# RWKV's sums over head channels on four groups of TensorE columns, and spreads through DRAM in place of matmuls

## The chip, the cores and the metric

The kernel runs on one core of a Trainium2 chip. The metric is the device time of one execution in microseconds (us). Below, PE is TensorE, DVE is VectorE, ACT is ScalarE, POOL is GpSimd and SP is SyncE, which here only issues DMAs. PEld is TensorE's loading of weights, which runs beside its matmuls.

## The reference

One decoder layer on x of 1024 tokens by 1024 channels, float32. After an RMS norm, one projection feeds two branches: an RWKV-7 time mixing (8 heads of 64 channels) and a sparse attention (8 heads of 64 channels, 256 keys for each query, chosen by an indexer). Their outputs are merged through sigmoid gates and followed by a SwiGLU FFN and a last norm. What the change touches:

```python
kk = (k * k_k).reshape(B, S, H, N)
kk = kk / jnp.maximum(jnp.linalg.norm(kk, axis=-1, keepdims=True), 1e-12)
...
bonus = jnp.sum(r_h * k_h * r_k, axis=-1, keepdims=True) * v_h
...
prob = jax.nn.softmax(logits, axis=-1)
return jnp.einsum('bqhk,bqkhd->bqhd', prob, vg)
```

The first is a sum of squares over the 64 channels of a head, for each token, whose inverse root multiplies all 64 channels again. The second is a sum over the same 64 channels that multiplies v's channels. The third divides the attention's output of a head by its softmax sum. All three are sums per head and token that have to be spread back over 64 channels. Channels lie on partitions here, two heads in each of four tiles of 128 channels, and tokens lie along the free dimension.

## The kernel before

Tokens are worked in two halves of 512; the RWKV branch works in four quarters of 256 tokens (q = 0 to 3, two in each half). Projections and FFN matmuls are float32 products made of three passes (mm3, L138, L139, L143): weights and activations are split into a high and a low part (split, L112 on ACT and L113 on DVE), and 24 matmuls of 512 columns make one output tile.

TensorE's order is written out by hand; the order on the other engines comes from the scheduler of the tile framework. A queue of generators, fill, holds the projection, gate, attention, merge and FFN work as small pieces; pump(n) takes n matmuls' worth of it and puts it into TensorE's queue at that place, so that it covers the latency of what stands around it. ticks(n, m) does the same in m parts. rwkv(half, ...) calls pump between its own steps with numbers for each quarter. In a quarter, in this order:

- L525 multiplies the decay and the in-context rate up, L529 takes their tanh on ACT, L536 scans the log decays on DVE, L540 and L542 exponentiate them on ACT (P and Pi).
- kk is scaled k, sq its square (L556). L561 sums sq over a head's channels: eight matmuls with sq as the stationary operand and the two-column indicator ind2 as the moving one, so that sums come with tokens on partitions. L564 bounds them from below, L566 raises them to the power -1/2 on POOL, L570 transposes them back (two transposes), L572 splits them into a high and a low part (nrT), and L579 spreads them over the channels with eight matmuls by the indicator ind8. L581 multiplies kk by the result in PSUM.
- L589 transposes v. AR (L597, L598) holds kk and r times decays, BK (L604, L607) the in-context rate times kk, and k, times inverse decays. rk (L612) is the product for the bonus.
- L622 sums and spreads rk at once, with the block matrix blk (128 by 128, ones where two channels are of one head); L623 multiplies v by the result in PSUM (bon).
- In q = 2, ready() then runs what is left of fill (the end of the attention of half 0), frees its buffers and puts the merge of half 0 into fill; the merge reads d_ya and d_yb back and splits them (L1095, L1096).
- L639 multiplies BK and AR into MT, L643 masks it on DVE, L658 transposes BK. Then follow a triangular solve on DVE, beside which ticks pumps fill, and the chunk recurrence; its end (finish) adds bon.

The attention (attend) works on units of a pair of heads and 128 queries. When a pair's four units are done, close1 takes the reciprocal of the softmax sums (ri), close2 spreads them over channels with eight matmuls against the identity (L1030) and copies the result to SBUF (L1033), and close3 multiplies the attention's output, still in PSUM, by it (L1037) and writes it to d_yb. close2 and close3 come one unit apart.

DMAs: SP carries RWKV's loads and stores and, outside RWKV, the weights; during RWKV the weights go through ACT's queue (wq). Each queue issues in order, and an issue that waits holds up those behind it.

Of the kernel before, what the change touches and what calls it, by code (L numbers as in the profile page):

```python
# [24 lines left out]
HT = 512  # L25
# [20 lines left out]
K_ID, K_ONE, K_CAUS, K_BO = range(4)  # L46
# [3 lines left out]
def block_kernel(ctx: ExitStack, tc: tile.TileContext, ins: dict, outT: bass.AP, stop=None, dbg=None):  # L50
# [30 lines left out]
    smp.tile([128, 40], F32, name="edge")  # L81
# [15 lines left out]
    d_yb = scratch("d_yb", [4, 128, HT])  # L97
    d_n = [dp.tile([64, 32, 32], F32, name=f"d_n{q}") for q in range(4)]
# [371 lines left out]
    def rwkv_consts(p):  # L470
        blk = p.tile([128, 128], F32, name="blk")
        SY.dma_start(blk, ins["consts"][:, K_BO, :])
# [6 lines left out]
        ind8 = p.tile([8, 512], F32R, name="ind8")  # L479
        t = tmp()  # L480
        SY.dma_start(t[0:8, :], ins["ind8"])
        A.activation(ind8, t[0:8, :], AF.Copy)
# [7 lines left out]
        ind2 = smp.tile([128, 2], F32, name="ind2")  # L490
        SY.dma_start(ind2, ins["ind2"])

        return blk, cmask, wup, gup, rmask, ind2, ind8

    def rwkv(half, p, consts, ready=None):
        blk, cmask, wup, gup, rmask, ind2, ind8 = consts
# [4 lines left out]
        for q in range(2 * half, 2 * half + 2):  # L501
# [43 lines left out]


# [10 lines left out]
            pump((30, 16, 16, 20)[q])  # L557
            ps = mix()
            for t in range(2):
                for ct in range(4):  # L560
                    T.matmul(ps[:, t * 8 + ct * 2:t * 8 + ct * 2 + 2], sq[:, ct, t * 128:(t + 1) * 128], ind2,  # L561
                             start=True, stop=True)
            nr = p.tile([128, 16], F32, tag="nr", name="nr")
            V.tensor_scalar(nr, ps[:, 0:16], 1e-24, None, op0=ALU.max)  # L564
# [4 lines left out]
            for t in range(2):  # L569
                T.transpose(ps[0:8, t * 128:(t + 1) * 128], nr2[:, t * 8:(t + 1) * 8], ident)  # L570
            nrT = p.tile([8, 2, 256], F32R, tag="rhs", name="nrT")
            split(nrT[:, 0, :], nrT[:, 1, :], ps[0:8, 0:256])  # L572
            pump(10)
            for c in range(2):
                ps = mix()
                for e in range(2):
                    ct = 2 * c + e
                    for i in range(2):
                        T.matmul(ps[:, e * 256:(e + 1) * 256], ind8[:, ct * 128:(ct + 1) * 128], nrT[:, i, :],  # L579
                                 start=i == 0, stop=i == 1)  # L580
                V.tensor_tensor(kk[:, 2 * c:2 * c + 2, :], kk[:, 2 * c:2 * c + 2, :],  # L581
                                ps.rearrange("p (c t) -> p c t", c=2), op=ALU.mult)
# [10 lines left out]

            kk4 = kk.rearrange("p c (n t) -> p c n t", n=4)
# [4 lines left out]
            V.tensor_scalar(ta, ta, 0.5, 0.5, op0=ALU.mult, op1=ALU.add)  # L599
            V.tensor_tensor(ta, ta, kk, op=ALU.mult)  # L600
            BK = [p.tile([128, 2, 2, 4, 64], F32, tag=f"BK{c}", name="BK") for c in range(2)]
            for c in range(2):
                s2 = slice(2 * c, 2 * c + 2)
                V.tensor_tensor(BK[c][:, :, :, 1:3, :].rearrange("p c r s t -> p (c r) (s t)"),  # L604
                                ta[:, s2, :].rearrange("p c (r t) -> p (c r) t", r=2),
                                Pi[:, s2, :].rearrange("p c (r t) -> p (c r) t", r=2), op=ALU.mult)
                V.tensor_tensor(BK[c][:, :, :, 0:4:3, :].rearrange("p c r s t -> p (c r) s t"),  # L607
                                km[:, s2, :].rearrange("p c (r s t) -> p (c r) s t", r=2, s=2),
                                Pi[:, s2, :].rearrange("p c (r s t) -> p (c r) s t", r=2, s=2), op=ALU.mult)
            rk = t4("x6")  # L610
            for ct in range(4):
                V.scalar_tensor_tensor(rk[:, ct, :], r[:, ct, :], par[:, P_RK + ct:P_RK + ct + 1], km[:, ct, :],  # L612
                                       op0=ALU.mult, op1=ALU.mult)


            bon = v
            pump((28, 38, 32, 32)[q])
            for c in range(2):
                ps = mix()
                for e in range(2):  # L620
                    ct = 2 * c + e
                    T.matmul(ps[:, e * 256:(e + 1) * 256], blk, rk[:, ct, :], start=True, stop=True)  # L622
# [333 lines left out]
    def attend(half, p, bias):  # L956
# [64 lines left out]
        def close1(sm):  # L1021
            ri = smp.tile([128, 4, 2], F32, tag="ri", name="ri", bufs=2)
            V.reciprocal(ri, sm)
            return ri

        def close2(ri):
            pb = mix()
            for bi in range(4):
                for e in range(2):
                    T.matmul(pb[64 * e:64 * e + 64, bi * 128:(bi + 1) * 128], ri[:, bi, e:e + 1].to_broadcast([128, 64]),  # L1030
                             ident, start=True, stop=True)
            rb = tmp()
# [383 lines left out]
```

## Time and profile before

| | |
|---|---|
| median of 3 runs | 1779.17 us (1772.55 to 1781.16) |
| the profiled execution | 1776.56 us, span 1774.8 us |
| mean granted clock of TensorE | 0.993 |
| instructions | 26838 |
| DMA | 244.00 MB, mean 137 GB/s |

The span runs from the first to the last instruction of the profiled execution; the execution's own time is a little longer. Busy time is the time in which an engine has at least one instruction under way. In the profile, a group or timeline row names the line of the kernel, the engine, the operation, what it writes and reads, the shape and the count; a bracket at the end of a timeline row tells how long the engine had been idle and which instruction released it. A float32 matmul stands in the profile as two records. Rows by window give, for each engine, its busy time and count, then TensorE's granted clock, the DMA engines' share and GB/s. In the rows of DMA issues the last number is the median time from issue to landing. In groups, the last column is the engine's idle time just before, and who ended it.

### The profile page before, as it was taken

The numbers are of one execution on the slowest core, as the hardware profiler recorded it, in microseconds if no ns is written. First come the engines' busy times: TensorE is split into PE (matmuls) and PEld (weight loads), VectorE is DVE, ScalarE is ACT, GpSimd is POOL, SyncE is SP. The second block draws the span as 40 slices with busy tenths as digits, with TensorE's granted clock in tenths as the row PEclk, the third lists the DMA queues.
The fourth block names the chain that finished last, engine by engine and source line by source line (L and its number), as shares of the span: only waits on it lengthen the run. The fifth ranks groups of instructions, "written<-read, shape, count | busy, mean of one in ns | idle before, by whom it ended". The sixth has DMA issues, their size and how long they took to land. (4 is left out here: it accounts for less than half of the span.)

```text
span 1774.8 us, 26838 instructions
## 1 busy us (share of the span) xinstructions
PE 1731.5 (98%) x10256; PEld 1432.1 (81%) x10256; DVE 1117.6 (63%) x2137; ACT 832.2 (47%) x1535; POOL 93.5 (5%) x120
## 2 busy tenths in 40 slices
PE   7999999999999999999999999999999999999997
PEld 6888888788888777777888888888788888888877
DVE  5779989866468568847865655524565564454464
ACT  6355998453444788654233455523334322232231
POOL 0000000010021110001000311000000000000000
PEclk9999999999999999999999999999999999999999
DMA  5542224536375535723244854243565344434441
GB/s 207 165 138 90 101 95 143 164 86 176 92 203 171 148 108 173 227 88 110 78 119 113 240 154 119 76 139 112 185 206 154 108 135 148 143 97 156 129 139 64
DMA packets 130992, 244.00 MB, mean 137 GB/s; under 512 B 36536, under 2 KB 59704, under 8 KB 130736
## 3 DMA queue, kind: packets, MB, share of 16 engines
q1 hardware_dynamic: 107472, 168.38, 30.7%
q10 hardware_dynamic: 15552, 47.75, 8.8%
q0 software_dynamic: 7840, 26.15, 5.6%
q8 instruction: 81, 1.33, 0.3%
q14 instruction: 47, 0.39, 0.1%
HBM read 189.29 MB, written 52.95 MB: 136 GB/s over the span
## 5 line engine op out<-in xcount | busy, mean ns | idle before, releaser
L113 DVE TENSOR_TENSOR wlo<-wst,whi 128x1024 fp32r<-128x1024 f32 (+1 forms) x231 | 277.8, 1204 | 306.1 <-PE acc L143 139.7
L112 ACT ACTIVATE whi<-wst 128x1024 fp32r<-128x1024 f32 (+1 forms) x231 | 240.6, 1043 | 282.3 <-PE acc L139 224.0
L138 PE MATMUL acc<-zhi,whi 128*128 128x512 f32 x672 | 265.8, 396 | 1.3 <-DVE tmp L1189 1.3
L139 PE MATMUL acc<-zlo,whi 128*128 128x512 f32 x672 | 262.8, 391 | 0.0
L143 PE MATMUL acc<-zhi,wlo 128*128 128x512 f32 x672 | 170.1, 392 | 0.0
L138 PEld LDWEIGHTS acc<-zhi,whi 128*128 128x128 f32 x672 | 126.8, 189 | 28.5 <-issue 3.4
L138 PE MATMUL acc<-fhi,whi 128*128 128x512 f32 (+1 forms) x400 | 145.0, 371 | 3.9 <-ACT fhi L112 3.9
L139 PEld LDWEIGHTS acc<-zlo,whi 128*128 128x128 f32 x672 | 126.8, 189 | 25.0
L143 PEld LDWEIGHTS acc<-zhi,wlo 128*128 128x128 f32 x672 | 124.8, 188 | 25.5 <-issue 0.7
L139 PE MATMUL acc<-flo,whi 128*128 128x512 f32 (+1 forms) x400 | 143.7, 367 | 1.4 <-DVE flo L113 1.2
L138 PE MATMUL acc<-u1hi,whi 128*128 128x512 f32 x352 | 140.5, 399 | 0.1
L138 PE MATMUL acc<-u0hi,whi 128*128 128x512 f32 (+1 forms) x352 | 135.3, 387 | 4.2 <-DVE tmp L281 2.4
L139 PE MATMUL acc<-u1lo,whi 128*128 128x512 f32 x352 | 137.6, 391 | 0.0
L139 PE MATMUL acc<-u0lo,whi 128*128 128x512 f32 (+1 forms) x352 | 133.7, 382 | 0.0
L143 PE MATMUL acc<-fhi,wlo 128*128 128x512 f32 (+1 forms) x400 | 92.6, 369 | 0.0
L138 PEld LDWEIGHTS acc<-fhi,whi 128*128 128x128 f32 x400 | 76.1, 190 | 17.9 <-ACT fhi L112 5.8
L143 PE MATMUL acc<-u1hi,wlo 128*128 128x512 f32 x352 | 89.7, 394 | 0.0
L139 PEld LDWEIGHTS acc<-flo,whi 128*128 128x128 f32 x400 | 76.2, 190 | 14.6 <-DVE flo L113 3.3
L143 PE MATMUL acc<-u0hi,wlo 128*128 128x512 f32 (+1 forms) x352 | 86.0, 384 | 0.0
L112 ACT ACTIVATE fhi<-tmp 128x512 fp32r<-128x512 f32 x44 | 27.8, 631 | 113.7 <-DVE tmp L1169 113.7
L138 PEld LDWEIGHTS acc<-u0hi,whi 128*128 128x128 f32 x352 | 66.1, 188 | 17.5 <-issue 2.6
L143 PEld LDWEIGHTS acc<-fhi,wlo 128*128 128x128 f32 x400 | 69.6, 191 | 12.1 <-issue 0.5
(304 smaller groups left out, 3146.0 us busy)
## 6 DMA issues: line engine op xcount, KB each, us to landing
wst<-in_w_ffn_in SPq DMA_DIRECT2D x72, 512.0 KB, 3.7
wst<-in_w_in ACTq DMA_DIRECT2D x36, 512.0 KB, 3.7
wst<-in_w_in SPq DMA_DIRECT2D x27, 512.0 KB, 3.7
wst<-in_w_fo SPq DMA_DIRECT2D x25, 512.0 KB, 3.7
k<-d_k POOLq DMA_DIRECT2D x24, 512.0 KB, 8.3
h<-in_xT SPq DMA_DIRECT2D x32, 256.0 KB, 5.2
d_g<-tmp ACTq DMA_DIRECT2D x32, 256.0 KB, 3.0
tmp<-d_g SPq DMA_DIRECT2D x32, 256.0 KB, 3.1
```

Of the source, the lines that this page charges most:

```text
L112: A.activation(hi, x, AF.Copy)
L113: V.tensor_tensor(lo, x, hi.bitcast(F32), op=ALU.subtract)
L138: T.matmul(ps, whi[:, wk + k, :], ahi[:, ak + k, tok], start=k == 0, stop=False)
L139: T.matmul(ps, whi[:, wk + k, :], alo[:, ak + k, tok], start=False, stop=False)
L143: T.matmul(ps, wlo[:, wk + k, :], ahi[:, ak + k, tok], start=False, stop=k == nk - 1)
```

## The change

Five things are done.

1. The sums over a head's channels, of sq and of rk, are made by one helper, sums(x): four matmuls with the indicator ind (128 by 32, two columns of which count) as the stationary operand, one for each tile of channels, into the rows 32 ct to 32 ct + 31 of one PSUM tile. So each uses its own 32 of TensorE's 128 columns.
2. The sums of sq are copied to SBUF (nq, on ACT), transposed by two matmuls, bounded and raised to the power on POOL as before, transposed again (16 rows), copied (nt), written to DRAM (d_kn) and read back with a broadcast over 64 partitions, once for each head parity, into the half of AR that isn't in use yet (nrs). One DVE instruction multiplies kk by nrs. AR's kk and r products come after it.
3. The sums of rk are copied to SBUF (bs), written to DRAM (d_bs), and read back with a broadcast into P's buffer once AR is made. One DVE instruction makes bon from v and it, and stands after the loads of the triangular solve.
4. In the softmax closing, close2 transposes ri (one matmul), copies it and the attention's output to SBUF and writes the sums to DRAM (d_s); a new close3 reads them back with a broadcast; close4 multiplies. So a closing takes three steps instead of two. The last pair of heads of half 0 keeps the matmuls.
5. The matmuls by ind2, ind8 and blk and the split of nrT are gone, ready() stands behind the sums of rk and ahead of AR, and the numbers of the pumps are others: a quarter pumps 16 more in all ahead of L639.

```diff
+            def sums(x):
+                ps = mix()
+                for ct in range(4):
+                    T.matmul(ps[32 * ct:32 * ct + 32, 0:256], ind, x[:, ct, :], start=True, stop=True)
+                return ps[:, 0:256]
...
             pump((30, 16, 16, 20)[q])
+            ps = sums(sq)
+            nq = p.tile([128, 2, 128], F32, tag="rhs", name="nq")
+            A.activation(nq.rearrange("p a b -> p (a b)"), ps, AF.Copy)
+            pump(4)
             ps = mix()
             for t in range(2):
-                for ct in range(4):
-                    T.matmul(ps[:, t * 8 + ct * 2:t * 8 + ct * 2 + 2], sq[:, ct, t * 128:(t + 1) * 128], ind2,
-                             start=True, stop=True)
+                T.transpose(ps[:, t * 128:(t + 1) * 128], nq[:, t, :], ident)
...
             G.tensor_tensor(nr2, nr, mhalf, op=ALU.pow)
             pump((34, 36, 30, 30)[q])
             ps = mix()
-            for t in range(2):
-                T.transpose(ps[0:8, t * 128:(t + 1) * 128], nr2[:, t * 8:(t + 1) * 8], ident)
-            nrT = p.tile([8, 2, 256], F32R, tag="rhs", name="nrT")
-            split(nrT[:, 0, :], nrT[:, 1, :], ps[0:8, 0:256])
-            pump(10)
-            for c in range(2):
-                ps = mix()
-                for e in range(2):
-                    ct = 2 * c + e
-                    for i in range(2):
-                        T.matmul(ps[:, e * 256:(e + 1) * 256], ind8[:, ct * 128:(ct + 1) * 128], nrT[:, i, :],
-                                 start=i == 0, stop=i == 1)
-                V.tensor_tensor(kk[:, 2 * c:2 * c + 2, :], kk[:, 2 * c:2 * c + 2, :],
-                                ps.rearrange("p (c t) -> p c t", c=2), op=ALU.mult)
+            T.transpose(ps[0:16, 0:128], nr2, ident)
+            nt = p.tile([16, 128], F32, tag="rhs", name="nt")
+            A.activation(nt, ps[0:16, 0:128], AF.Copy)
+            SY.dma_start(d_kn[q].rearrange("e c (t s) -> (e c t) s", t=2), nt)
+            nrs = AR.rearrange("p c n s t -> p (c n s t)")[:, 1024:2048]
+            for e in range(2):
+                SY.dma_start(nrs[64 * e:64 * e + 64, :],
+                             d_kn[q][e].rearrange("c s -> (c s)").partition_broadcast(64))
...
+            rk = t4("x6")
...
+            pump((10, 12, 10, 10)[q])
+            bs = tmp()
+            A.activation(bs[:, 0:256], sums(rk), AF.Copy)
+            for e in range(2):
+                SY.dma_start(d_bs[q][e], bs[e::32, 0:256])
+            if q == 2:
+                ready()
...
+            V.tensor_tensor(kk.rearrange("p c t -> p (c t)"), kk.rearrange("p c t -> p (c t)"), nrs, op=ALU.mult)
             kk4 = kk.rearrange("p c (n t) -> p c n t", n=4)
...
-            pump((28, 38, 32, 32)[q])
-            for c in range(2):
-                ps = mix()
-                for e in range(2):
-                    ct = 2 * c + e
-                    T.matmul(ps[:, e * 256:(e + 1) * 256], blk, rk[:, ct, :], start=True, stop=True)
-                V.tensor_tensor(bon[:, 2 * c:2 * c + 2, :], v[:, 2 * c:2 * c + 2, :],
-                                ps.rearrange("p (c t) -> p c t", c=2), op=ALU.mult)
-
-            if q == 2:
-                ready()
+            pump((40, 48, 44, 44)[q])
...
+            bsp = t4("P")
+            for e in range(2):
+                SY.dma_start(bsp[64 * e:64 * e + 64].rearrange("p c t -> p (c t)"),
+                             d_bs[q][e].rearrange("c s -> (c s)").partition_broadcast(64))
+            bon = v
+            V.tensor_tensor(bon, v, bsp, op=ALU.mult)
             ticks((255, 240, 285, 245)[q], (13, 4, 10, 6)[q])
...
+            T.transpose(pb[0:8, 0:128], ri.rearrange("p e b -> p (e b)"), ident)
+            y = p.tile([128, HT], F32, tag="y", name="y")
+            rt = tmp()
+            A.activation(rt[0:8, 0:128], pb[0:8, 0:128], AF.Copy)
+            A.activation(y, py, AF.Copy)
+            SY.dma_start(d_s[half][hp].rearrange("e (b t) -> (e b) t", b=4), rt[0:8, 0:128])
+            return None, y
+
+        def close3(x, hp):
+            rb, y = x
+            if rb is None:
+                rb = tmp()
+                for e in range(2):
+                    SY.dma_start(rb[64 * e:64 * e + 64, :], d_s[half][hp][e].partition_broadcast(64))
+            return rb, y
```

More of the change, by code (lines that the diff above doesn't have):

```diff
@@ L43 @@
 NPAR = 66
-K_ID, K_ONE, K_CAUS, K_BO = range(4)
+K_ID, K_ONE, K_CAUS = range(3)
 @with_exitstack
@@ L1021, in close1 @@
         def close1(sm):
-            ri = smp.tile([128, 4, 2], F32, tag="ri", name="ri", bufs=2)
-            V.reciprocal(ri, sm)
-            return ri
-        def close2(ri):
-            pb = mix()
-            for bi in range(4):
-                for e in range(2):
-                    T.matmul(pb[64 * e:64 * e + 64, bi * 128:(bi + 1) * 128], ri[:, bi, e:e + 1].to_broadcast([128, 64]),
-                             ident, start=True, stop=True)
-            rb = tmp()
-            A.activation(rb, pb, AF.Copy)
-            return rb
@@ L1036, in close3, with close2 @@
-        def close3(rb, py, hp):
-            V.tensor_tensor(rb, py, rb, op=ALU.mult)
-            SY.dma_start(d_yb[half][hp], rb)
+            ri = smp.tile([128, 2, 4], F32, tag="ri", name="ri", bufs=2)
+            V.reciprocal(ri.rearrange("p e b -> p b e"), sm)
+            return ri
+        def close2(ri, py, hp):
+            pb, rb = mix(), None
+            if half == 0 and hp == 3:
+                for bi in range(4):
+                    for e in range(2):
+                        T.matmul(pb[64 * e:64 * e + 64, bi * 128:(bi + 1) * 128],
+                                 ri[:, e, bi:bi + 1].to_broadcast([128, 64]), ident, start=True, stop=True)
+                rb = tmp()
+                A.activation(rb, pb, AF.Copy)
+                return rb, py
+            T.transpose(pb[0:8, 0:128], ri.rearrange("p e b -> p (e b)"), ident)
[5 more added lines that the diff above has]
+            return None, y
```

73 lines of the change are left out of this document (37 added, 36 removed).

## Prediction

> **What bounds the kernel now.** I read the page first, for its busy shares and its chain.
>
> ```profile
> span 1774.8 us, 26838 instructions
> PE 1731.5 (98%) x10256; PEld 1432.1 (81%) x10256; DVE 1117.6 (63%) x2137; ACT 832.2 (47%) x1535; POOL 93.5 (5%) x120
> PE 25%; issue 1%; DVE 1%; DMA 1%; ACT 0%; POOLq 0%; POOL 0%; DVEq 0%; ACTq 0%
> ```
>
> TensorE is busy for 98% of the span, and the part of the chain that could be followed back is TensorE too. Its order is written out by hand, and the projection matmuls (the fill) keep it busy between other steps. So the whole time is TensorE's work plus the time in which it waits. A matmul taken out of its queue is a gain of its own length, and each microsecond in which the head of its queue waits is lost. The other engines count only where TensorE waits for them.
>
> **What TensorE no longer does.** Next I read TensorE's timeline around the touched steps of the second quarter (q = 1); the columns are start, length, engine, line.
>
> ```profile
> 510.70 0.39 PE L139 MATMUL acc<-u1lo,whi 128*128 128x512 f32 x1
> ...
> 511.61 0.39 PE L139 MATMUL acc<-u1lo,whi 128*128 128x512 f32 x1
> 511.83 1.84 PE L561 MATMUL mix<-ind,AR 128*128 128x2 f32 x16
> 513.53 0.49 PE L138 MATMUL acc<-u1hi,whi 128*128 128x512 f32 x1
> ```
>
> ```profile
> 521.84 0.38 PE L570 MATMUL mix<-kc,nr 128*8 128x128 f32 x2
> 521.98 1.17 PE L143 MATMUL acc<-u1hi,wlo 128*128 128x512 f32 x4
> ...
> 524.88 1.09 PE L579 MATMUL mix<-nrT,ind 8*128 8x256 f32 x7 [0.53 <-DVE nrT L113]
> 525.90 1.09 PE L589 MATMUL mix<-kc,v 128*128 128x128 f32 x8
> 526.75 0.47 PE L138 MATMUL acc<-u1hi,whi 128*128 128x512 f32 x1
> ```
>
> ```profile
> 535.33 1.89 PE L622 MATMUL mix<-x,blk 128*128 128x256 f32 x8
> 537.15 4.29 PE L639 MATMUL mix<-AR,BK 64*128 64x128 f32 x64
> 541.37 1.97 PE L658 MATMUL mix<-kc,BK 128*128 128x128 f32 x16
> 543.09 0.48 PE L138 MATMUL acc<-u1hi,whi 128*128 128x512 f32 x1
> ```
>
> Lengths overlap in the pipeline, so I count from start to start. A fill matmul takes 0.91/4 = 0.228. L561 takes 1.70, L570 0.14, L579 1.02 for 7 and so 1.17 for 8, L622 1.82: 4.83 us in a quarter go. What comes is three transposes (two like L589's, 0.85/8 = 0.106 each, one like L570's, 0.07; 0.28 together) and two sums, of k squared and of rk, on four column groups. One sum has the records of L622: 8 of 256 columns. No row shows four groups; the softmax spread shows two.
>
> ```profile
> 575.95 1.04 PE L1030 MATMUL mix<-kc,ri 128*64 128x128 f32 x16
> 576.92 0.74 PE L993 MATMUL mix<-k,q 128*128 128x512 f32 x2
> ```
>
> 16 records of 128 columns take 0.97, 0.061 each, against half of L622's 0.228, 0.114, with no groups: two groups work almost twice as fast. A sum then costs between 1.82/4 = 0.46 and 1.82 (no overlap at all). I take 0.96, the speed of the nearest row. A quarter saves 4.83 - 1.92 - 0.28 = 2.63, four save 10.5 (3.6 to 14.5). Seven of eight softmax closings replace L1030 by one transpose: 7 x (0.97 - 0.07) = 6.3. **Term a: -16.8** (-20.8 to -9.9).
>
> [...] Ahead of and behind L1030's two-group run the starts above hide at most about 0.1 us each; 16 such borders would be 1.6 us, inside the bounds of term a.
>
> **Waits that go.** TensorE's groups by line, then three stretches of 3.4 us in the last quarter:
>
> ```profile
> L579 PE MATMUL mix<-nrT,ind 8*128 8x256 f32 x32 | 6.4, 331 | 3.0 <-DVE nrT L113 2.9 <-ACT nrT L112 0.2
> L138 PE MATMUL acc<-yhi,whi 128*128 128x512 f32 x128 | 50.7, 396 | 3.3 <-ACT yhi L112 2.0 <-DVE h L1189 1.3
> L658 PE MATMUL mix<-kc,BK 128*128 128x128 f32 x64 | 8.4, 279 | 0.7 <-DVE MT L643 0.7
> ```
>
> ```profile
> 840.50:843.90 3.40, 1.50 (x6) 0.76 (x5) 3.40 (x6) 1.07 (x3) 0.00 (x0) 1.00 0.07 27
> 843.90:847.30 3.40, 3.18 (x14) 2.96 (x15) 2.92 (x7) 0.24 (x1) 0.00 (x0) 0.50 0.54 157
> 847.30:850.70 3.40, 3.40 (x11) 2.72 (x10) 3.40 (x6) 2.13 (x4) 0.00 (x0) 0.50 0.02 5
> ```
>
> The split of nrT goes, and its 3.0 us of waiting. In the stretches TensorE is busy for 1.50 of 3.40 us (the long wait for nrT), and the clock granted after it is 0.50 for two stretches: about 3.2 us more. **Term b: -6.2** (to 0, if other waits put the clock down there).
>
> **New wait 1: the copy of the sums (nq).** TensorE must transpose nq four fill matmuls (0.91) after the sums. The copy stands in ScalarE's queue, and in the changed kernel's order it stands behind both exponentials of the decay (L540, L542), which wait for VectorE's scans. Before, nothing on TensorE waited for these. VectorE's, then ScalarE's timeline in the first quarter, where the old sums (L561) started at 359.8:
>
> ```profile
> 358.27 2.43 DVE L536 TENSOR_TENSOR_SCAN x<-rmask,x 128x256 f32<-128x256 f32 x4
> ```
>
> ```profile
> 360.74 1.06 ACT L540 ACTIVATE P<-x 128x1024 f32<-128x1024 f32 x1 [1.74 <-DVE x L536]
> 361.70 1.04 ACT L542 ACTIVATE x<-x 128x1024 f32<-128x1024 f32 x1
> 362.65 0.60 ACT L427 ACTIVATE stg<-mix,rsk 128x128 f32<-128x128 f32 x2
> 363.15 0.41 ACT L517 ACTIVATE wa<-wa 64x256 f32<-64x256 f32 x1
> 363.46 1.05 ACT L112 ACTIVATE whi<-wst 128x1024 fp32r<-128x1024 f32 x1
> ```
>
> The new order puts nq behind all five: it starts at 364.5 and, at 0.4 for this size (L517), ends at 364.9. TensorE is there at 359.8 + 0.96 + 0.91 = 361.7: a wait of 3.2. In the other quarters only the two exponentials and at most one short step stand in front; with the scans as late as here, nq ends near 363.3, so about 2 us each. **Term c: +9** (0, if the scans come earlier, to 16, 4 us in each quarter, if one more split of weights of 1.05 stands in front).
>
> **New wait 2: the round trip of the norms.** After the transpose of nr2 come a copy on ScalarE, a write to DRAM, two broadcast reads on the same SP queue, then VectorE's kk, four AR products, ta and two BK products; only then can L639 start. Landing times, then VectorE's groups:
>
> ```profile
> k<-d_k POOLq DMA_DIRECT2D x24, 512.0 KB, 8.3
> tmp<-d_g SPq DMA_DIRECT2D x32, 256.0 KB, 3.1
> N<-d_n SPq DMA_DIRECT2D x8, 256.0 KB, 4.0
> d_n<-MT SPq DMA_DIRECT2D x32, 32.0 KB, 1.6
> ```
>
> ```profile
> L597 DVE TENSOR_TENSOR AR<-x,P 128x512 f32<-128x512 f32 x8 | 5.2, 687 | 0.1
> L600 DVE TENSOR_TENSOR x<-x,x 128x1024 f32<-128x1024 f32 x4 | 4.9, 1218 | 0.0
> L604 DVE TENSOR_TENSOR BK<-x,x 128x512 f32<-128x512 f32 x8 | 5.2, 686 | 0.1
> ```
>
> Copy and issues 1.6 (estimate: one short ScalarE step and three SP issues), write 1.6, read 3.5 (between 3.1 and 4.0), kk 1.2, AR 2.7, ta 1.2, BK 1.4: 13.2 us. TensorE's work between is, in q = 0, L589 0.85, sums 0.96, 48 fill matmuls 10.9 and 8 transposes 0.85: 13.6, so no wait. In q = 1 it is about 13, and the new order puts one split of weights and two softmax steps into VectorE's chain: +3. In q = 3 it is 14.6 with one split and a product in the chain: +1. The bonus product waits for its own broadcast between the masks of L643, about 0.5 in each of three quarters. **Term d: +5.5** (0, with reads at 3.1 and nothing between, to 16, with reads at 8.3 in all three).
>
> **New wait 3: the join in q = 2.** ready() now stands ahead of the chain above, and after it come 44 fill matmuls, the first of the merge. They need d_ya and d_yb read back and split. Before, this stood between L1030 and that merge:
>
> ```profile
> 677.42 1.09 PE L1030 MATMUL mix<-kc,ri 128*64 128x128 f32 x16
> 678.44 1.99 PE L622 MATMUL mix<-x,blk 128*128 128x256 f32 x8
> 680.36 5.00 PE L639 MATMUL mix<-AR,BK 64*128 64x128 f32 x64
> ```
>
> That was 10 us of cover (L658 included), with 2.0 + 0.7 us of waiting left. In the new order VectorE has kk and the AR products, waiting for the norms, ahead of the first split of y; SP has the bonus broadcast, which waits for the AR products to let go of P, ahead of all four reads of d_yb. Counted from the transpose of nr2, TensorE reaches the merge at 0.85 + 0.97 + 0.96 = 2.8; the splits start at 1.6 + 1.6 + 3.5 + 1.2 + 2.7 = 10.6, so the first product can run near 11.3. The d_yb reads also wait for the four temporary buffers that the splits of d_ya let go, at 0.69 each (L597's size) with ta between: 10.6 + 1.2 + 2.8 = 14.6, 3.1 to land and 0.7 for the split, near 18 for the last. TensorE has 12 matmuls (2.7) before it needs the first of them and 12 that use all four. I take 12 us of waiting, less 2.7 before. **Term e: +9.3** (3, if SP and VectorE get past early, to 14).
>
> **The clock.** Five new waits of 2 us or more can each be followed by 3.4 us at 0.50, 1.7 us, as the stretches show; a wait of this length doesn't always do it, so I take half for four and all of the join's. **Term f: +4.5** (0 to 9). [...]
>
> **The sum.** -16.8 - 6.2 + 9 + 5.5 + 9.3 + 4.5 = +5.3. The profiled execution took 1776.56; the runs' median is 1779.17, 2.6 higher. So 1781.9 on its scale and 1784.5 on that of the median: no change that can be told, since about 0.5% (8.9 us) is what a measurement of this kernel can tell.
>
> **Rivals.**
> - Savings win: ScalarE and SP get to the small copies early. c is 3, d 0, e 5 and f 1: -14, 1765. For it: VectorE is 63% and ScalarE 47% busy. Against it: their order is fixed, and the exponentials and the AR products stand in front.
> - Slower: the broadcast reads, 64 partitions from one row, land like k<-d_k, 8.3, not 3.5. Since work and chain are level at 13.6 and 13.2, every microsecond past that counts in full: 4.8 us in four quarters, +19, 1803. It decides from a landing of about 4 us on. For it: DRAM reads here range from 3.1 to 8.3. Against it: SP's reads of 256 KB all stay near 4.
> - The four groups don't overlap: eight sums of 1.82, not 0.96: +6.9, 1791. Against it: L1030.
>
> **Chances.** Forecast 0.48 (own range 1776 to 1793), savings win 0.20, slow reads 0.24, no overlap 0.08. Below 1770.3 lie most of the second and a trace of the first: 0.20. Between the bounds lie 0.30 of the first and 0.05 of the others: 0.35. Above 1788.1: 0.45. The range 1765 to 1802 leaves out half of the savings' case and about 0.1 at the top.
>
> **What would show it.** In the changed profile: the four-group matmuls at about 1 us per sum; TensorE waiting for ScalarE's nq for 2 to 3 us at each pair of transposes; L639 waiting for BK by 0 to 3 us; at q = 2 some 12 us of waiting for ylo and yhi at the merge; stretches of clock 0.50 after these. Wrong would be: no wait at nq (c falls), reads landing past 5 us (d), or a merge that starts within 5 us (e).

## The result and the profile after

The changed kernel takes 1795.44 us (median of 4 runs, 1792.55 to 1799.47) against 1775.96 for the kernel before in the same measurement: ratio 1.0109 (95% interval 1.007 to 1.0147). Measured again beside other runs it gave 1794.92, ratio 1.0093 (1.0073 to 1.0114). It is slower by about 1%: inside the range on record, beyond the forecast's own range. The profiled execution took 1797.63.

The page of the changed kernel: the span, the busy line, and the chain of work that ended last.

```profile
span 1795.8 us, 26586 instructions
PE 1723.2 (96%) x10091; PEld 1420.5 (79%) x10091; DVE 1116.4 (62%) x2125; ACT 835.4 (47%) x1549; POOL 92.5 (5%) x120
PE 70%; DVE 12%; ACT 8%; DMA 5%; issue 4%; SPq 0%; POOL 0%; DVEq 0%; ACTq 0%; POOLq 0%
```

TensorE has fewer instructions and the span is 21.0 longer, so TensorE waits more: outside its busy time lie 72.6 us, before 43.3. DVE, ACT and DMA stand in the chain with 25% together; the two chains can't be compared share by share, since the one before could be followed back for little more than a quarter of the span. What TensorE's head of queue waited for (us in total, times, longest):

```profile
PE mix L567 <- ACT nq L563: 11.5, 4, 6.8
PE acc L141 <- ACT yhi L115: 10.0, 3, 8.3
...
PE mix L639 <- ACT L L1005: 5.6, 1, 5.6
...
PE mix L639 <- DVE MT L643: 3.6, 2, 3.3
...
PE acc L142 <- DVE ylo L116: 1.4, 5, 0.4
...
PE mix L639 <- DVE BK L624: 1.1, 1, 1.1
```

These are the three kinds of new waits: the copy of the sums (L567), the norms' and the bonus's way through DRAM (L639), the join in the third quarter (L141, L142). The 5.6 that stand under ACT L belong to the norms: L639 needs the first product of BK too, and that ended 0.1 us before L639 went on.

Busy time needs one more division, since a matmul at half clock is busy for twice as long: in the timeline below, a fill matmul takes 0.39 us at full clock (519.78) and 0.78 at half (527.82). By the trace's clock records TensorE was busy at half clock for 20.3 us before and for 45.1 after. Half of that is counted as lost, so a span is made of three parts: work at full clock (busy time less that half), what half clock costs, and the rest, idle.

| profiled execution | span | work at full clock | lost at half clock | idle |
|---|---|---|---|---|
| before | 1774.8 | 1721.4 | 10.1 | 43.3 |
| changed | 1795.8 | 1700.7 | 22.5 | 72.6 |
| difference | +21.0 | -20.7 | +12.4 | +29.3 |

**The second quarter** shows how a wait comes about. The changed kernel's timeline, TensorE first, then ScalarE, POOL's and SP's queues:

```profile
518.87 0.64 PE L546 MATMUL mix<-AR,ind 128*32 128x256 f32 x8
519.44 0.50 PE L141 MATMUL acc<-u1hi,whi 128*128 128x512 f32 x1
519.78 0.39 PE L142 MATMUL acc<-u1lo,whi 128*128 128x512 f32 x1
...
527.48 0.69 PE L567 MATMUL mix<-kc,nq 128*128 128x128 f32 x2 [6.84 <-ACT nq L563]
527.82 0.78 PE L141 MATMUL acc<-u1hi,whi 128*128 128x512 f32 x1
...
524.85 0.42 ACT L513 ACTIVATE wa<-wa 64x256 f32<-64x256 f32 x1 [6.59 <-DMA wa<-d_rw]
...
525.18 1.04 ACT L536 ACTIVATE P<-x 128x1024 f32<-128x1024 f32 x1
526.12 1.04 ACT L538 ACTIVATE x<-x 128x1024 f32<-128x1024 f32 x1
527.07 0.36 ACT L563 ACTIVATE nq<-mix 128x256 f32<-128x256 f32 x1
...
511.61 1.29 POOL L974 DMA_DIRECT2D k<-d_k  x2 [13.70 <-PE acc L146]
512.90 0.77 POOL L978 DMA_DIRECT2D v<-d_v  x1
513.66 2.41 POOL L986 DMA_DIRECT2D q<-d_q  x4
...
515.12 0.34 SPq L502 DMA_DIRECT2D wa<-d_rw  x1
```

Read it backwards. The transposes (L567) wait for nq. nq takes 0.36, but in ScalarE's queue it stands behind two exponentials, and these behind a tanh (L513) that belongs to the next quarter and waits 6.59 us for its load. That load is 128 KB and was issued at 515.12, amid POOL's loads for the attention; the tanh that it released starts 9.7 us later. Before, the sums came with tokens on partitions, so that no copy by ScalarE stood between them and the power. From start to start the sum takes 0.57 (518.87 to 519.44), against 1.82 for as many records without groups (L622 before), so the four groups do run side by side.

**The join** in the third quarter, by windows of 3.41 us (columns: PE, PEld, DVE, ACT, POOL busy, then granted clock, DMA share, GB/s):

```profile
704.75:708.16 3.41, 0.00 (x0) 0.00 (x0) 0.69 (x1) 3.16 (x9) 0.00 (x0) 1.00 0.91 291
708.16:711.57 3.41, 0.00 (x0) 0.00 (x0) 3.10 (x5) 2.40 (x9) 0.00 (x0) 0.50 0.89 249
711.57:714.98 3.41, 2.60 (x4) 1.26 (x5) 3.41 (x6) 3.41 (x9) 0.00 (x0) 0.50 0.74 240
714.98:718.39 3.41, 3.41 (x9) 2.64 (x9) 3.08 (x8) 3.33 (x9) 0.00 (x0) 0.50 0.84 272
```

TensorE stands still for 8.3 us, and when it starts again it runs at half clock until 718.39. So the wait is paid for again: 6.0 us of matmuls run at half clock here, of which 3.0 are lost.

### The profile page after: what moved, and what is told of

The parts are those of the page before. It is cut to its first block, busy times and chain, and to the rows that moved or that the text cites. A ratio compares the mean times of both kernels' runs of the same rounds, so it can differ in the third digit from the quotient of the medians.

```text
span 1795.8 us, 26586 instructions
## 1 busy us (share of the span) xinstructions
PE 1723.2 (96%) x10091; PEld 1420.5 (79%) x10091; DVE 1116.4 (62%) x2125; ACT 835.4 (47%) x1549; POOL 92.5 (5%) x120
## 4 chain that ended last, share of the span: by engine, by line
PE 70%; DVE 12%; ACT 8%; DMA 5%; issue 4%; SPq 0%; POOL 0%; DVEq 0%; ACTq 0%; POOLq 0%
PE acc L141 18%; PE acc L142 18%; PE acc L146 18%; DVE wlo L116 2%; PE mix L1024 2%; PE mix L1000 2%; ACT junkl L915 2%; ACT junk L915 2%; PE mix L1014 1%; PE mix L867 1%; ACT whi L115 1%; DVE junk L912 1%; PE mix L772 1%; PE mix L760 1%; DMA tmp<-d_yb 1%
## 5 line engine op out<-in xcount | busy, mean ns | idle before, releaser
L141 PE MATMUL acc<-zhi,whi 128*128 128x512 f32 x672 | 264.4, 393 | 0.0
L142 PE MATMUL acc<-zlo,whi 128*128 128x512 f32 x672 | 261.9, 390 | 0.0
L141 PE MATMUL acc<-fhi,whi 128*128 128x512 f32 (+1 forms) x400 | 146.3, 374 | 4.2 <-ACT fhi L115 4.2
L141 PEld LDWEIGHTS acc<-zhi,whi 128*128 128x128 f32 x672 | 126.2, 188 | 27.2 <-issue 2.0
L142 PEld LDWEIGHTS acc<-zlo,whi 128*128 128x128 f32 x672 | 126.2, 188 | 25.0
L142 PE MATMUL acc<-flo,whi 128*128 128x512 f32 (+1 forms) x400 | 143.8, 368 | 1.2 <-DVE flo L116 1.2
L141 PE MATMUL acc<-u1hi,whi 128*128 128x512 f32 x352 | 143.5, 408 | 0.1
L142 PE MATMUL acc<-u1lo,whi 128*128 128x512 f32 x352 | 140.2, 398 | 0.0
L141 PE MATMUL acc<-u0hi,whi 128*128 128x512 f32 (+1 forms) x352 | 135.0, 386 | 4.2 <-DVE tmp L284 2.4
L142 PE MATMUL acc<-u0lo,whi 128*128 128x512 f32 (+1 forms) x352 | 133.7, 383 | 0.0
L141 PEld LDWEIGHTS acc<-fhi,whi 128*128 128x128 f32 x400 | 76.3, 191 | 18.7 <-ACT fhi L115 6.1
L142 PEld LDWEIGHTS acc<-flo,whi 128*128 128x128 f32 x400 | 76.4, 191 | 13.6 <-DVE flo L116 2.7
L141 PEld LDWEIGHTS acc<-u1hi,whi 128*128 128x128 f32 x352 | 68.0, 193 | 15.4 <-issue 1.6
L141 PEld LDWEIGHTS acc<-u0hi,whi 128*128 128x128 f32 x352 | 66.2, 188 | 17.5 <-issue 2.6
```

Of the source, the lines that this page charges most:

```text
L141: T.matmul(ps, whi[:, wk + k, :], ahi[:, ak + k, tok], start=k == 0, stop=False)
L142: T.matmul(ps, whi[:, wk + k, :], alo[:, ak + k, tok], start=False, stop=False)
```

## The experiments

**Theory W**: the work saved is real, and the loss is TensorE waiting at the new places, with the half clock behind them. Its rivals: the softmax closings (S), the DRAM traffic by itself (C), the place of the join (J), the bonus product (B). Runs 1 to 4, 5 to 8, 9 to 11 and 12 are four groups, each on one chip with runs of the kernel before beside it; across groups the ratios are compared. All of them, with the three parts of their profiled executions:

| kernel | median | ratio to before (95%) | work | half clock | idle |
|---|---|---|---|---|---|
| 1 RWKV part only | 1797.23 | 1.0098 (1.0072 to 1.0123) | 1708.0 | 20.3 | 68.8 |
| 2 norms at once | 1786.18 | 1.0049 (1.0032 to 1.0067) | 1699.1 | 21.7 | 67.7 |
| 3 nq first | 1787.6 | 1.0052 (1.0031 to 1.0072) | 1700.7 | 20.8 | 65.8 |
| 4 join late | 1800.33 | 1.0118 (1.0084 to 1.0152) | 1698.8 | 29.8 | 79.5 |
| 5 bonus only | 1788.14 | 1.006 (1.0041 to 1.0078) | 1717.7 | 14.0 | 53.3 |
| 6 changed again | 1794.92 | 1.0093 (1.0073 to 1.0114) | 1700.7 | 25.1 | 69.1 |
| 7 tanh behind | 1788.15 | 1.0055 (1.0034 to 1.0076) | 1701.4 | 14.6 | 64.2 |
| 8 first mending | 1793.26 | 1.0087 (1.0069 to 1.0105) | 1700.9 | 26.0 | 64.0 |
| 9 bonus late | 1786.77 | 1.0048 (1.0031 to 1.0066) | 1700.1 | 19.1 | 65.5 |
| 10 bonus only, late | 1774.46 | 0.998 (0.9962 to 0.9998) | 1719.5 | 5.0 | 43.3 |
| 11 no norms | 1769.7 | 0.995 (0.9932 to 0.9967) | 1714.4 | 10.2 | 45.0 |
| 12 second mending | 1782.91 | 1.0032 (1.0015 to 1.0049) | 1698.9 | 19.8 | 65.7 |

The work column repeats within 3 us between kernels with the same matmuls. A profiled execution can lie up to 10 us off its kernel's median (1809.85 in run 4, 1781.98 in run 7), so small differences of the other two columns say little.

**1. Softmax closings by matmuls again**

```diff
-            if half == 0 and hp == 3:
+            if True:
```

> All softmax closings spread by matmuls again, as before the change; only the RWKV part of the change is left. Theory W (the loss is TensorE's waiting at the new places in RWKV, and the clock that falls behind these waits; the softmax part is a gain of 6.3 us, seven closings of 0.90 each): 1801 us, that is 4 to 8 us above the changed kernel's 1795.4. Rival S (the softmax closings' way through DRAM costs more than the matmuls that it saves, through its late products and the copy of y): at least 5 us below the changed kernel, 1790 or less.

1797.23, ratio 1.0098, and the changed kernel at 1.0109 and 1.0093: no difference that can be told. The loss of 5 us that S expected isn't seen, nor the gain that W expected; the intervals are too wide to exclude the lower end of either. The work shows the saving (1708.0 against 1700.7, 7.3 less with the softmax part). Half clock and idle take it back; in the changed kernel, for one, a stretch of 10.2 us at half clock begins at 626, in this one it is 3.4 us.

**2. Nobody waits for the norms' write**

```diff
-                             d_kn[q][e].rearrange("c s -> (c s)").partition_broadcast(64))
+                             ins["nfix"][e].partition_broadcast(64))
```

> The two broadcast reads of the norms read a constant row of the same size, not what was just written; so kk isn't divided by its norm (the sums, the copies and the write stay, and every transfer stays, but nobody waits for the write). Theory W: L639's waits of the second and last quarter (5.6 and 1.1) go, VectorE gets to the splits of y earlier and the join of the third quarter falls from 8.3 to 2 to 5, and with it some half clock: 1783 us (1778 to 1788), some 12 below the changed kernel. The wait for nq (11.5 in all) stays. Rival C (the added traffic to and from DRAM slows the kernel, not the waiting for it): no change, 1793 to 1798, since the traffic is the same.

This kernel leaves out the division of kk by its norm. 1786.18, some 9 below the changed kernel, inside W's range and below C's. With as many bytes moved, about half of the loss goes, so that half isn't the amount of traffic. L639 waits for nothing any more, and the join's first wait falls from 8.3 to 3.8, though a second one of 3.3 follows it. But a wait for nq of 5.4 comes up in the first quarter, where there was 0.2: the steps that are freed take their places in the queues ahead of others. There the product of kk (L615) starts at 357.73, ahead of the sums, after VectorE has stood still for 6.99 us for its read. So the reads also moved to other times, and what they cost where they stood isn't settled by this run.

**3. nq first on ScalarE**

```diff
+            with tc.high_priority():
-            A.activation(nq.rearrange("p a b -> p (a b)"), ps, AF.Copy)
+                A.activation(nq.rearrange("p a b -> p (a b)"), ps, AF.Copy)
```

> The copy of the sums (nq) goes ahead on ScalarE's queue: in the second quarter ahead of the second exponential and of the tanh that waits for its load, in the third ahead of both exponentials. Theory W: the waits for nq of 6.8 and 3.6 become under 1 each; the exponentials come 0.4 later, which nobody on TensorE waits for; about 10 us of waiting and about 2 of half clock go, some of it comes back at L639: 1785 us (1781 to 1790). Rival D (the chain behind the norms is what ends last in these quarters, and the wait for nq only stands in front of it): the time moves to L639, 1793 to 1798.

1787.6: about the time W gave, by another way than it said. The third quarter's wait of 3.4 for nq went, the second's stayed at 6.0, since nq still stood behind the tanh that waits for its load. L639's wait in that quarter went down instead, from 5.6 to 3.1.

**4. The join behind the fill**: the two lines of ready() moved from behind the sums of rk to behind pump((40, 48, 44, 44)[q]).

> ready(), which queues the merge's products, stands behind the 40 to 48 fill matmuls ahead of L639, not ahead of the chain of the norms. Theory W: in the third quarter too little fill is left to cover the chain of the norms, so the 8.3 us of waiting at the merge become 8 to 10 us at L639: no change against the changed kernel, 1791 to 1800. Rival J (the place of the join is itself the loss): the wait at the merge goes and none takes its place, 1783 to 1788.

1800.33, just above W's range. J is out: the wait at the merge went and one of 11.2 us came at L639 in its place, somewhat more than W expected; fill was used up there. The join is short of cover at both places.

**5. The bonus part alone**, on the kernel before; norms and closings by matmuls as they were.

```diff
-                    T.matmul(ps[:, e * 256:(e + 1) * 256], blk, rk[:, ct, :], start=True, stop=True)
+                T.matmul(ps[32 * ct:32 * ct + 32, 0:256], ind, rk[:, ct, :], start=True, stop=True)
...
+            bsp = t4("P")
...
+            V.tensor_tensor(bon, v, bsp, op=ALU.mult)
```

> The kernel before with the bonus part alone: the sum of rk on four column groups, its spread through DRAM; norms and softmax closings as before, the merge joined where it was. Theory W: four sums save 4 x (1.82 - 0.85) = 3.9 us on TensorE, the bonus product between the masks costs 0 to 4 us of waiting at L639 with the clock behind it: 1774 to 1780, within 0.3% of before. Then the whole loss of the changed kernel hangs on the norms and the join. Rival B (the bonus product between the masks, with its broadcast that waits for P, is a main part of the loss, as the wait of 3.3 us in the first quarter suggests): 1783 or more.

1788.14, inside B's range: this small part, which W had put at 0 to 4 us of waiting, costs 10 us alone. VectorE's timeline and the windows of the second quarter in this kernel:

```profile
537.00 1.29 DVE L643 TENSOR_TENSOR MT<-mix,cmask 128x512 f32<-128x512 f32 x2 [1.69 <-PE mix L639]
542.35 1.23 DVE L700 TENSOR_TENSOR v<-v,P 128x1024 f32<-128x1024 f32 x1 [4.06 <-DMA P<-d_bs]
543.49 3.73 DVE L643 TENSOR_TENSOR MT<-mix,cmask 128x512 f32<-128x512 f32 x6
```

```profile
538.00:541.00 3.00, 0.97 (x17) 0.78 (x14) 0.29 (x1) 0.00 (x0) 0.00 (x0) 1.00 0.94 318
541.00:544.00 3.00, 0.00 (x0) 0.00 (x0) 1.65 (x2) 0.00 (x0) 0.00 (x0) 0.88 0.15 25
544.00:547.00 3.00, 2.77 (x18) 2.55 (x19) 3.00 (x6) 0.00 (x0) 0.00 (x0) 0.50 0.19 31
```

The bonus product isn't needed before the end of the quarter, but the scheduler put it between the masks (L643). VectorE stands still for 4.06 us until the broadcast lands; six masks stand behind it in the queue, TensorE stops in the middle of L639 for 5.3 us for want of them, and goes on at half clock (0.50 from 544.00 to 547.00).

**6. The changed kernel again**, for the comparison with 1.

> The changed kernel itself once more, on the same chip as the runs beside it, as the point that they are compared with: 1795 (1791 to 1799). It also gives what the softmax part is worth, against the run with the RWKV part alone: theory W said 4 to 8 us, that run stood at 1.0098 of before, so W needs this one at 1.0075 or less; at 1.009 or more the softmax part gives back most of what it saves.

1.0093 lies above the 1.009 set there, by far less than its interval (1.0073 to 1.0114). It points to a softmax part that, as it stands in the changed kernel, gives back most of what it saves, and doesn't prove it.

**7. The tanh behind nq**: run 3, and wa shares a buffer with gd, so that its load is issued earlier.

```diff
+            wg = p.tile([128, 2, 256], F32, tag="wg", name="wg")
...
-                t = p.tile([128, n, 256], F32, tag=tag, name=tag)
+                t = (p.tile([128, n, 256], F32, tag=tag, name=tag) if n > 1 else
+                     wg[:, 0:1, :] if tag == "wa" else wg[:, 1:2, :])
```

> nq ahead on ScalarE's queue as in the third run, and wa shares its buffer with gd, so that its load is issued with gd's, ahead of the attention's loads of 2.4 MB, and its tanh no longer stands ahead of nq in the second quarter. Theory W: the wait of 6 us for nq in the second quarter goes with its half clock, about 8 us below the third run: 1779 (1775 to 1784). Rival D (the loads that saturate the DMA engines or the norms' chain hold that quarter anyway): the wait moves to L639 or to the products of wa, 1785 to 1790.

1788.15, inside D's range and no better than run 3. The wait for nq in the second quarter went (6.0 to 0.8), but idle time fell by 1.6 only: the waits for ylo now come to 4.4, against 1.5 in run 3, and L639 waits 4.2 in the second quarter, against 3.1. The next waits took back most of what that one gave.

**8. All of it with more cover**: the edits of 3 and 7, the bonus product on GpSimd, the join as in 4, and fill moved ahead of L639.

```diff
-            V.tensor_tensor(bon, v, bsp, op=ALU.mult)
+            G.tensor_tensor(bon, v, bsp, op=ALU.mult)
...
-            pump((40, 48, 44, 44)[q])
+            pump((50, 72, 60, 60)[q])
+            if q == 2:
+                ready()
...
-            ticks((255, 240, 285, 245)[q], (13, 4, 10, 6)[q])
+            ticks((190, 216, 269, 229)[q], (13, 4, 10, 6)[q])
```

> The whole change, with its waits taken away: nq ahead and wa with gd as in the run beside it, the bonus product on GpSimd, the merge joined behind the fill matmuls ahead of L639, and 12, 24, 16, 16 more fill matmuls there, taken from the stretch behind (65, 24, 16, 16 fewer). Theory W: what is left is the saving on TensorE, 13 to 17 us, less some 5 of small waits: 1766 (1761 to 1772), below the kernel before. Rival C (traffic to DRAM and half clock from other waits are what costs, not these places): 1780 or more. Rival F (the fill that is taken from behind the masks is missed there, where TensorE waits for the inverse): 1773 to 1782.

1793.26: a miss for W, by 27 us. The second quarter again: SP's queue and VectorE, then the windows.

```profile
515.71 0.34 SPq L583 DMA_DIRECT2D d_kn<-nt  x1
522.82 1.12 SPq L586 DMA_DIRECT2D AR<-d_kn  x2
...
534.13 1.23 DVE L617 TENSOR_TENSOR x<-x,AR 128x1024 f32<-128x1024 f32 x1 [12.03 <-DMA AR<-d_kn]
```

```profile
521.00:524.00 3.00, 3.00 (x15) 2.49 (x14) 1.10 (x2) 0.80 (x3) 0.51 (x1) 1.00 1.04 362
524.00:527.00 3.00, 3.00 (x15) 2.49 (x14) 0.00 (x0) 0.99 (x1) 0.25 (x1) 1.00 1.03 240
527.00:530.00 3.00, 3.00 (x16) 2.54 (x16) 0.00 (x0) 0.00 (x0) 0.00 (x0) 1.00 1.03 287
530.00:533.00 3.00, 1.77 (x9) 1.31 (x7) 0.00 (x0) 0.00 (x0) 0.00 (x0) 1.00 1.00 298
```

The quarter comes earlier in this kernel, so the round trip of the norms falls among the attention's loads, and the DMA engines are at a share of 1.00 to 1.04 from 521 to 533. Between 512 and 534 us two reads of 256 KB on SP's queue stand among 3.1 MB on POOL's. From the issue of the write (515.71) to kk (L617, 534.13) it takes 18.4 us; in the changed kernel, where the quarter comes later, 10.4 (538.86 to 549.23). VectorE stands still for 12.03 us with the attention's logits queued behind, and TensorE waits 11.0 for the exponential that follows them. So C has a point that its wording missed: here the cost is not traffic as such, but two transfers at one time, one of which somebody waits for.

That isn't the whole miss. F shows too: behind the solves, where fill had been taken away, TensorE waits 4.8 us in the second quarter and 2.5 in the third, and a stretch of 13.7 us at half clock begins at each place (607 and 774). The two hold 25.8 us of matmuls, so 12.9 are lost. How the 27 us divide between the two causes this run doesn't tell.

**9. The bonus product behind the solve**: the broadcast goes into N's buffer, which comes free only when the solve is done.

```diff
-            bsp = t4("P")
+            bsp = t4("x6")
```

> The changed kernel, with the broadcast of the bonus sums read into the buffer of N (x6), free only when the triangular solve is done, so that VectorE's bonus product stands behind the solve and no longer among the masks. Theory B (new since the run with the bonus part alone, 1.006 of before: VectorE stands still in its queue for that broadcast, and TensorE for the masks): the wait of 3.4 us in the first quarter, the 1 us waits in the others and the half clock behind them go: 1789 (1785 to 1792), some 6 below the changed kernel. Rival N (only the norms, nq and the join count here, the masks' wait is covered by the next wait): 1793 or more. Rival X (the late read or product delays the inverse that TensorE waits for behind the ticks): 1797 or more.

1786.77, ratio 1.0048: some 8 below the changed kernel (B had said 6), by one word. No wait for MT of over 0.2 us is left.

**10. The bonus part alone, behind the solve**: run 5 with the same word changed.

> The bonus part alone, as in the fifth run, with the same late broadcast. Theory B: its saving of 3.7 us on TensorE stays and the waits of 5.3 and 2.9 behind the masks go with their half clock, so 10 to 14 below the fifth run's 1788: 1774 (1770 to 1779), at or below the kernel before. Rival C (four-group matmuls amid the fill, or the traffic of the spread, cost by themselves): 1784 or more, with no wait to show for it.

1774.46, ratio 0.998 (0.9962 to 0.9998). Between runs 5 and 10 lie 13.7 us, with the same matmuls and the same bytes, so the loss of run 5 comes neither from the four-group matmuls nor from the traffic by itself, but from where the product stands. Idle is 43.3, what it was before.

**11. The bonus behind the solve and the second half's closings through DRAM**: run 10, with close2 to close4 of the changed kernel and this condition.

```diff
-            if half == 0 and hp == 3:
+            if half == 0:
```

> The bonus part with the late broadcast, the softmax closings of the second half through DRAM (four of eight), and the norms and the join as in the kernel before. Theory B with W: TensorE's work is 3.7 and 4 x 0.95 shorter, and no step that TensorE waits for goes through DRAM: 1770 (1766 to 1775), some 8 below the kernel before. Rival S (the softmax closings give back what they save, as the pair of runs with and without them suggests): 1773 to 1778, no lower than the bonus part alone.

1769.7, ratio 0.995 (0.9932 to 0.9967): faster than both kernels, and what W with B said. Its longest waits on TensorE are those of the kernel before:

```profile
PE acc L364 <- ACT u0hi L256: 6.6, 1, 6.6
PE acc L140 <- ACT fhi L114: 4.5, 5, 1.9
PE mix L230 <- DVE sacc L224: 2.8, 2, 1.6
PE mix L581 <- DVE nrT L115: 2.6, 3, 2.0
```

Four closings in the second half took the ratio from 0.998 to 0.995 (the intervals overlap a little), while seven in both halves gave nothing that could be told in runs 1 and 6. That it is the first half's three which give it back, where RWKV's steps stand in the same queues, is argued from this and not shown by itself.

**12. The whole change mended otherwise**: 3, 4, 7 and 9 together, with the fill for it taken from the second quarter.

```diff
-            ticks((255, 240, 285, 245)[q], (13, 4, 10, 6)[q])
+            ticks((255, 200, 285, 245)[q], (13, 4, 10, 6)[q])
```

> The whole change with its waits mended, but the attention's loads and the norms' chain of the second quarter left in the order that they have in the seventh run: nq ahead, wa with gd, the bonus broadcast late, the merge joined behind the fill matmuls ahead of L639, with 40 fill matmuls of cover for them taken from the stretch behind the masks of the second quarter (240 to 200). Against the seventh run (1.0055 of before) Theory W with B takes away the join's waits (7.8 and 2.8), the masks' 2.0 and about 6 us of half clock, and adds some 3 us behind the second quarter's solve: 1773 (1768 to 1778), that is 0.997 of before, or no lower than the run without the norms (1769.7), since L639's wait in the second quarter (4.3) stays. Rival R (the norms' round trip is not to be covered in this kernel: wherever fill is put in front of it, it is missed behind the masks): 1780 or more.

1782.91: W missed by 10 us, and R's 1780 or more holds. What TensorE waits for in it:

```profile
PE mix L643 <- DVE BK L626: 12.9, 3, 6.6
...
PE mix L711 <- DVE TZ L697: 6.5, 3, 5.5
```

L643 (the old L639) waits 12.9 us for the norms' chain after all, in three quarters, and the fill that was taken is missed behind the solve (L711): 5.5 us at 598.58, and 20.5 us at half clock that begin at 597. Against run 11 TensorE has 15.5 us less work, 20.7 more idle time and 9.6 more of half clock: the norms by DRAM, with the first half's closings, lose where bonus and second-half closings win. No run has the norms alone or the first half's closings alone, so the two aren't parted, and whether some other arrangement of the attention's loads would carry the norms wasn't tried.

## Why the prediction came out as it did

Its kinds of cost were right; their sum was 16 us short on the profile's scale: +5.3 against +21.0. That the time still lies inside 1765 to 1802 is owed to the width of that range, which the rivals had set, and not to the sum. Term by term:

- **Term a, TensorE's work**: -16.8, measured -20.7, at the end of its bounds. One sum on four groups took 0.57 from start to start, with 0.11 lost behind it (519.44 to 519.78, where a fill matmul takes 0.228; the prediction had about 0.1 for such a border), not 0.96: the nearest row had two groups, and four are faster still. No overlap of groups, a rival, is refuted by L546.
- **Term b, the waits that go**: the 3.0 for nrT went, and the half clock behind it in the last quarter too. Right.
- **Term c, the wait for nq**: +9, measured 11.5. The total is near by luck, for the parts aren't: they are 0.2, 6.8, 3.4 and 1.0, where 3.2, 2, 2 and 2 were forecast. In the first quarter the first exponential started 2.7 us earlier (358.06 against 360.74); in the second nq waits for a load, which the prediction's row of ScalarE in the first quarter could not show.
- **Term d, the norms' round trip and the bonus**: +5.5, measured 10.3 (10.6 at L639 and 0.9 at L658, less 0.5 and 0.7 before). Among the waits its size was worst. In the second quarter L639 waits 5.6, not 3, and not for the steps in VectorE's chain that the prediction named:

```profile
537.42 0.27 PE L576 MATMUL mix<-kc,nr 128*16 128x128 f32 x1
538.86 0.34 SPq L579 DMA_DIRECT2D d_kn<-nt  x1
542.01 1.13 SPq L582 DMA_DIRECT2D AR<-d_kn  x2
549.23 1.23 DVE L615 TENSOR_TENSOR x<-x,AR 128x1024 f32<-128x1024 f32 x1 [4.64 <-DMA AR<-d_kn]
```

From the transpose of nr2 (L576) to kk (L615) it takes 11.8 us, where 1.6 + 1.6 + 3.5 = 6.7 were forecast, and VectorE stands still for the last 4.64 of it. The bonus product was put at 0.5 in each of three quarters, 1.5; the masks' waits are 4.5, against 1.0 before, and alone (run 5) it lifted idle time by 10.0. That wait stands in VectorE's queue ahead of masks that feed TensorE, and it was priced as a short delay, not as the landing of two reads of 256 KB.

- **Term e, the join**: +9.3, measured 8.2 (9.8 at L141 and L142 between 711 and 722, less 1.6 at the merge before; of the 2.7 that the prediction subtracts, 1.1 stand elsewhere, behind 1275). The size was right. Of the chain, VectorE's part came as forecast: its first split of y (ylo) starts 11.5 us behind the transpose of nr2, where 10.6 was forecast. But the wait was ended by ScalarE's split (yhi), which went ahead when the first read of d_ya landed, issued on SP at 707.51 only, behind the end of the attention. Run 4 shows that the place of the join isn't the cost.
- **Term f, the clock**: +4.5, with 3.2 of term b going the other way, so +1.3 net; measured +12.4. This is the step that failed. Each of the five new waits of over 3 us (3.3, 6.8, 5.6, 3.4, 8.3) brought a stretch of 6.8 to 10.2 us at half clock. TensorE was busy for 25.3 us in these, so they cost 12.6. The prediction's own rows (843.90 and 847.30) show two stretches of 3.4 us behind a wait of 2.0, and term b counts both as 3.2; term f counted one for each new wait, and that with a chance of a half for four of them. (Half of 1.7 for four and the whole for the join also makes 5.1, not 4.5; the sum would be +5.9.) Another 4.6 were lost in the stretch that begins at 626, ahead of which TensorE waits for no more than 1.4 us at once: its rows are in the last section. Stretches of the kernel before that went make up the difference.

So the misses are 11.1 on the clock, 8.5 on idle time (c 2.5, d 4.8, e -1.1, and 2.3 elsewhere), less 3.9 on the work: 15.7. The rival with slow reads (a landing of 8.3, 1803) was wrong as a rule for the changed kernel; what was held against it, that SP's reads of 256 KB all stay near 4, was too narrow, for before they had medians from 2.8 (tmp<-d_h) to 5.2 (h<-in_xT). The medians of the landings are

```profile
AR<-d_kn SPq DMA_DIRECT2D x8, 256.0 KB, 4.6
P<-d_bs SPq DMA_DIRECT2D x8, 256.0 KB, 4.0
```

but the trace knows only one of the eight landings in the first row and two in the second. kk, which the read releases in every quarter, starts 4.0, 6.7, 5.0 and 4.3 us behind the issue of the second read: all above the 3.5 that was forecast, and in the second quarter past the 5 us that the prediction had named as a sign against itself. Run 8 shows the rival at work as soon as the reads meet the attention's loads (10.7 in its second quarter). The savings' rival is refuted for the whole change; for two of its three parts, placed otherwise, runs 10 and 11 show that the saving can be had.

## What to carry to other kernels

Here a matmul that was replaced by a round trip through DRAM saved its own length and put a transfer's landing into the queues that touch it: 10.4 us from the norms' write to kk in the second quarter, 18.4 in run 8 at a DMA share of 1.0, with VectorE's queue at a stand for 4.64 and 12.03 of these. So do it only for results that nobody needs soon, and let the consumer stand behind the last urgent instruction of its engine. One buffer's name decided 14 us (runs 5 and 10). Where TensorE is the bound, price a new wait at its length and the half clock that comes with it: here five waits of 27.4 us together brought 12.6 us more.

## What the runs showed of the hardware

In these two traces the clock falls on a grid of 3.41 us, and not by idle time alone. In the kernel before, stretches at half clock begin at 762.01, 813.21, 843.93 and 1280.84 us: the last three lie 51.20, 81.92 and 518.83 behind the first, which is 15, 24 and 152 times 3.413. Three windows of this kernel, then two of the changed one, the first number after the comma being TensorE's busy time (they start some 0.25 us behind the grid, hence clocks such as 0.97 and 0.53):

```profile
738.36:741.77 3.41, 2.21 (x10) 1.74 (x10) 2.27 (x10) 2.31 (x7) 0.00 (x0) 1.00 0.98 366
...
758.84:762.25 3.41, 2.93 (x83) 2.56 (x83) 0.33 (x1) 2.55 (x5) 0.00 (x0) 0.97 0.02 5
762.25:765.66 3.41, 3.41 (x14) 2.27 (x12) 0.68 (x3) 0.72 (x2) 0.00 (x0) 0.53 0.00 0
```

```profile
623.05:626.46 3.41, 2.58 (x80) 2.31 (x80) 0.85 (x2) 3.25 (x9) 0.00 (x0) 0.96 0.40 145
626.46:629.87 3.41, 2.31 (x9) 1.61 (x8) 1.93 (x4) 3.37 (x10) 0.00 (x0) 0.50 0.01 1
```

With 1.20 us idle among 10 matmuls of full size the clock stayed (738.36); with 0.48 or 0.83 idle (0.48 and 1.01 on the grid itself) among 80 small ones, most of them 32 by 32, it fell. What decides it, these rows don't settle.
